# Attention branch rebuilt around half-wide tables, keys and norm pairs, and GpSimd's mixer arithmetic on VectorE

## The chip, the cores and the metric

One core of one Trainium2 chip runs the whole program. The metric is the device time of one execution in microseconds (us); lower is better. In the profile PE is TensorE, DVE is VectorE, ACT is ScalarE, POOL is GpSimd and SP is SyncE, which issues the DMAs.

## What is computed

A trunk of two layers over 1024 tokens of width 1024, all in float32. Cut to what matters here:

```python
z = rmsnorm(h, g_attn) @ w_in           # one projection, feeds three mixers
a = gmlp(z[0:512])                      # chunked, 4 heads
b = attention(q=z[512:1024], k, v)      # 8 query heads, 2 key heads, window 128, sinks
c = s5_ssm(z[1280:1536])                # complex scan, then a gated unit
h = h + concat(norm(a), norm(b), norm(c)) @ w_out
h = h + relu(rmsnorm(h, g_mlp) @ w_ff1)**2 @ w_ff2
h = h + sigmoid(rmsnorm(h, g_ple) @ w_ple_gate) * (p[i] @ w_ple_proj)

def attention(q, k, v):
    q, k = rope(rmsnorm(q, gq)), rope(rmsnorm(k, gk))
    s = masked(q @ k.T / 8)             # the block's own 128 keys and the 128 before
    m = max(max(s), sink)
    pr = exp(s - m)
    return (pr / (sum(pr) + exp(sink - m))) @ v
```

## The kernel before

The 1024 tokens are worked on as two halves (h = 0, 1) of 512. A stage set (l, h) is layer l of half h: `project`, then the three mixers `attention`, `ssm` and `gmlp`, then `mix_out` (the w_out product, L1182), then the window. `window(l, h)` (L1218) is the channel MLP followed by the product with w_ple_gate; between the two it calls `embedding` (L1305), which loads and transposes p. Every wide product runs as three passes over values split in two parts (hi and lo); `load_w` (L93) makes such a pair of weights: a DMA into `st`, a cast on ACT (L104) and a subtraction on DVE (L105). `split_scaled` (L87) makes a pair of activations: ACT writes hi (L89), DVE writes lo (L90).

The stages are generators (`lane`). While a window issues its own matmuls through `main`, the lanes are stepped a fixed number of times per matmul, so that the mixers of the next stage set but one are written into the program between the matmuls of the window (`mix_lane`, L1409). The `until` at L1245 runs the lanes of the next stage set to their end before the second half of the window's last chunk (the w_ff2 product of chunk 7) and `embedding` are written. Tile then orders the instructions of each engine (L1436); on the chip each engine works strictly in that order.

Before the first window there is no such cover. `run` (L1384) projects half 0, starts `gmlp(0,0)` and `attention(0,0)`, projects half 1 as the main work, and finishes `mix_out(0,0)`, which needs all three mixers of half 0. The last reduction of the queries' squares in the projection of half 1 is L685. `early=3` lets three outputs of that `mix_out` begin with the parts that are ready.

`attention` (L946): per block of 128 tokens `rope` builds its two tables from the gains (L992), multiplies by the root and rotates (L993 to L1000), keys in `k_steps`, queries in `q_steps`. A unit is a block and a key head: `attn_q` transposes its queries, `attn_scores`, `attn_softmax`, `attn_pt` and `attn_pv` follow. `attn_norm` (L1158) sums the squares of a finished block on DVE (L1167), adds over partitions with a matmul (L1169), forms the root on DVE in steps of 128 columns (L81 to L85) and multiplies on POOL (L1173); `attn_out` writes the pair of halves into X. `rstd_wide` (L270) is the other way to a root: a matmul with ones, two DVE steps, three rounds of one ACT square and two DVE steps (L281 to L283), all reading a PSUM bank. Its default bank `o` also holds `po` of attention and one of the two `ppt` tiles of `embedding` (L1309).

Of the kernel before, what the change touches and what calls it, by code (L numbers as in the profile page):

```python
# [62 lines left out]
class Trunk:  # L63
# [206 lines left out]
    def rstd_wide(self, sq, count, eps, key, scratch, tag="o"):  # L270


        V, ps = self.V, self.bank(tag)
# [4 lines left out]
        a = pool.tile([P, 512], F32, tag=t, name="rs_a", bufs=bufs)
# [5 lines left out]
        self.R[key] = (None, y)  # L284
# [66 lines left out]
    def setup(self):  # L351
# [42 lines left out]
        self.hf = B.tile([P, 2, 4, 10], F32, name="hf")  # L394
        self.carry = B.tile([P, 2, 2, 4, 1], F32, name="carry")
# [12 lines left out]
    def load_gains(self, t):  # L408
# [9 lines left out]
        Q.dma_start(self.sinks.rearrange("p l a -> p (l a)"), a["sinks"].rearrange("l a -> (l a)").partition_broadcast(P))  # L418

# [249 lines left out]
    def project(self, l, h, ring, tag, one_pass):  # L669
# [35 lines left out]
        self.rsqrt(f, s2, self.small, 40)  # L705
        self.flags.add(("zq", l, h))
# [17 lines left out]
    def ssm(self, l, h, side, tag="p"):  # L724
# [17 lines left out]
        def states(gh):  # L742
# [14 lines left out]
            for ri, (x1, x2, op) in enumerate(((sr, si, ALU.add), (si, sr, ALU.subtract))):  # L757
# [3 lines left out]
                G.tensor_tensor(d1[:, ri, :, 1:65], d1[:, ri, :, 1:65], tm[:, :, 0:64], op)  # L761
# [64 lines left out]
        G.tensor_tensor(gw[:, 1], raw, gw.bitcast(F32)[:, 0], ALU.subtract)  # L826
# [25 lines left out]
        for m in range(2):  # L852
            G.tensor_tensor(yc[m], yc[m], self.R["t"][1], ALU.mult)
# [8 lines left out]
    def gmlp(self, l, h, side, tag="p", after=()):  # L862
# [28 lines left out]
        G.tensor_tensor(x, x, bc(mu), ALU.subtract)  # L891
# [19 lines left out]
        G.tensor_tensor(vg, vg, lng.unsqueeze(1).to_broadcast([P, 4, 256]), ALU.mult)  # L911
        G.tensor_tensor(vg, vg, lnb.unsqueeze(1).to_broadcast([P, 4, 256]), ALU.add)
# [24 lines left out]
        for m in range(2):  # L937
            G.tensor_tensor(u[:, m], u[:, m], self.R["t"][1], ALU.mult)
# [7 lines left out]
    def attention(self, l, h, side):  # L946
# [4 lines left out]
        c = dict(l=l, h=h, at=at, kts={}, qs={}, seen=-1, b0=b0)  # L951
        kv = at.tile([P, nb, 2, 2, 64], F32, name="kv")
        for i in range(nb):
            b = b0 + i
            Q.dma_start(kv[:, i].rearrange("p x a d -> p (x a d)"), self.zg[l][b // 4][b % 4][:, 256:512])
        c["kv"] = kv

        gs = []
        for i, (nm, sc) in enumerate((("q_norm_g", 0.125), ("k_norm_g", 1.0))):
            gt = at.tile([P, 2, 2, 32], F32, name=f"g{i}")  # L960
            g, s = gt[:, 0], gt[:, 1]
# [25 lines left out]
    def rope(self, c, x, f, i, b, n):  # L987

        V, G, at = self.V, self.G, c["at"]
        ta, tb = (at.tile([P, 2, 32], F32, name=f"t{j}", bufs=2) for j in range(2))  # L990
        for t, g, cs in zip((ta, tb), c["gains"][i], (self.cos, self.sin)):
            G.tensor_tensor(t, g, cs[:, b].unsqueeze(1).to_broadcast([P, 2, 32]), ALU.mult)  # L992
        G.tensor_tensor(x, x, f.unsqueeze(2).to_broadcast([P, n, 64]), ALU.mult)  # L993
        t1 = at.tile([P, n, 2, 32], F32, tag="rt1", name="rt1")
        t2 = at.tile([P, n, 2, 32], F32, tag="rt2", name="rt2")
        xb = x.rearrange("p h (a d) -> p h a d", a=2)
        G.tensor_tensor(t1, xb, ta.unsqueeze(1).to_broadcast([P, n, 2, 32]), ALU.mult)
        for s in range(2):
            V.tensor_tensor(t2[:, :, s], xb[:, :, 1 - s], tb[:, s].unsqueeze(1).to_broadcast([P, n, 32]), ALU.mult)
        V.tensor_tensor(xb, t1, t2, ALU.add)  # L1000

    def k_steps(self, c):

        V, S, G, T, at = self.V, self.S, self.G, self.T, c["at"]
        for i in range(c["kv"].shape[1]):
            b = c["b0"] + i
            k = c["kv"][:, i, 0]
            self.rope(c, k, self.hf[:, b // 4, b % 4, 8:10], 1, b, 2)
            kst = at.tile([P, 2, 2, 2, 64], F32R, name="kst")
            hi = kst[:, :, 0, 0]  # L1010
            S.copy(hi, k)
            V.tensor_tensor(kst[:, :, 0, 1], k, hi.bitcast(F32), ALU.subtract)
            V.tensor_tensor(kst[:, :, 1, 0], k, hi.bitcast(F32), ALU.subtract)
            S.copy(kst[:, :, 1, 1], k)
            yield
            pk = self.ps.tile([P, 512], F32, tag="t", name="pk")
            for j in range(4):
                T.matmul(pk[:, j * P:(j + 1) * P], kst[:, j // 2, j % 2].rearrange("p a d -> p (a d)"), self.identr,
                         start=True, stop=True)

            kt = at.tile([P, 2, 2, 2, P], F32R, name="kt", bufs=2)
            S.copy(kt[:, :, :, 1], pk.rearrange("p (g s c) -> p g s c", g=2, s=2))
            if i:
                S.copy(kt[:, :, :, 0], c["kts"][b - 1].bitcast(F32)[:, :, :, 1])
            c["kts"][b] = kt

    def q_steps(self, c):
        qs = []

        def load():  # L1030
            q = c["at"].tile([P, 8, 64], F32, name="q", bufs=2)
# [4 lines left out]
        load()  # L1036
        yield
        for i in range(4):
            self.rope(c, qs[i], self.hf[:, c["h"], i, 0:8], 0, 4 * c["h"] + i, 8)
            c["qs"][4 * c["h"] + i] = qs[i]  # L1040
            if 0 < i < 3:
                load()
            yield

    def attn_steps(self, c, kl, ql):

        h, at = c["h"], c["at"]
# [27 lines left out]
        while late:  # L1075
            blk = late.pop(0)[1]
            self.attn_out(c, blk, o.pop(blk))

    def attn_q(self, c, blk, gk):
        V, S, T, at = self.V, self.S, self.T, c["at"]  # L1080
        qh = c["qs"][blk][:, gk * 4:gk * 4 + 4]
        qst = at.tile([P, 4, 2, 64], F32R, name="qst")
        S.copy(qst[:, :, 0], qh)
# [356 lines left out]
```

## Time and profile before

| what | value |
|---|---|
| median of 3 runs | 2416.62 us (2414.51 to 2419.43) |
| the profiled execution | 2412.62 us, span 2410.8 us, granted clock 0.991 |
| PE busy | 2333.5 us, 97% of the span, 10957 instructions |
| DVE busy | 1604.0 us, 67% |
| ACT busy | 1025.4 us, 43% |
| POOL busy | 288.7 us, 12%, 313 instructions |
| DMA queue of SP | 39.4% of 16 engines' span |

The profile is of one execution. Busy time is a sum over the whole span; a stage can have another limit than the whole. An idle time in front of an instruction is listed with the event that ended it. The row of the granted clock tells at which of its levels TensorE ran.

### The profile page before, as it was taken

To read this page: it belongs to the slowest core of one execution; us is meant where nothing else is said; L and a number is where in the kernel's file an instruction comes from. 1 tells how busy PE (TensorE), PEld (TensorE's weight loads), DVE (VectorE), ACT (ScalarE), POOL (GpSimd) and SP (SyncE) were. 2 spreads that over 40 slices of the span, in tenths; PEclk is the share of its full clock that TensorE was granted. 3 is DMA by queue.
4 is the path that set the end of the run, shared out by engine and by line. 5 is a ranking of instruction groups with operands and counts; after the bars stand their busy time and mean duration, and the time that the engine had idled before them with its cause. 6 is when DMAs were issued, how large, how long until landed. Compare 5 with 4: busy or idle time off the path is not lost. (4 is left out here: it accounts for less than half of the span.)

```text
span 2410.8 us, 29899 instructions
## 1 busy us (share of the span) xinstructions
PE 2333.5 (97%) x10957; PEld 1882.7 (78%) x10957; DVE 1604.0 (67%) x2741; ACT 1025.4 (43%) x1813; POOL 288.7 (12%) x313
## 2 busy tenths in 40 slices
PE   7879999999999999999999999999999999999999
PEld 6656777887788887778788787778878878888887
DVE  7899798658666647876766764777575754444464
ACT  7357465334344434643433543553343533222242
POOL 0642321101000003211010001311010000000000
PEclk9989999999999999999999999999999999999999
DMA  7665522534533244234333335325343333333232
GB/s 236 191 184 149 158 82 79 162 97 139 158 96 114 89 148 127 83 111 148 111 124 102 103 111 152 108 71 162 99 122 115 102 103 109 97 97 96 88 114 71
DMA packets 407212, 289.71 MB, mean 120 GB/s; under 512 B 74668, under 2 KB 384792, under 8 KB 405272
## 3 DMA queue, kind: packets, MB, share of 16 engines
q1 hardware_dynamic: 407064, 287.78, 39.4%
q8 instruction: 87, 1.43, 0.2%
q14 instruction: 61, 0.50, 0.1%
HBM read 252.58 MB, written 35.15 MB: 119 GB/s over the span
## 5 line engine op out<-in xcount | busy, mean ns | idle before, releaser
L104 ACT CAST w<-st 128x1024 fp32r<-128x1024 f32 x384 | 410.4, 1070 | 841.7 <-PE mm_ps L344 441.2
L344 PE MATMUL mm_ps<-x,w 128*128 128x512 f32 x2736 | 666.7, 396 | 10.4 <-DVE hss L685 3.8
L105 DVE TENSOR_TENSOR w<-st,w 128x1024 fp32r<-128x1024 f32 x384 | 494.0, 1288 | 188.5 <-ACT w L104 181.9
L344 PEld LDWEIGHTS mm_ps<-x,w 128*128 128x128 f32 x2736 | 513.7, 189 | 129.0 <-issue 13.8
L344 PE MATMUL mm_ps<-A,w 128*128 128x512 f32 x2016 | 505.3, 394 | 4.2 <-DVE H L1228 3.0
L344 PEld LDWEIGHTS mm_ps<-A,w 128*128 128x128 f32 x2016 | 375.4, 188 | 90.4 <-issue 5.5
L344 PE MATMUL x_ps<-A,w 128*128 128x512 f32 x1056 | 276.7, 395 | 4.8 <-DVE H L1228 3.6
L344 PE MATMUL s_ps<-x,w 128*128 128x512 f32 x1056 | 253.4, 391 | 4.5 <-DVE w L105 3.2
L344 PEld LDWEIGHTS x_ps<-A,w 128*128 128x128 f32 x1056 | 195.7, 188 | 52.8 <-DVE H L1228 7.6
L344 PEld LDWEIGHTS s_ps<-x,w 128*128 128x128 f32 x1056 | 197.7, 188 | 49.6 <-DVE w L105 4.9
L344 PE MATMUL x_ps<-x,w 128*128 128x512 f32 x960 | 232.3, 392 | 0.0
L344 PEld LDWEIGHTS x_ps<-x,w 128*128 128x128 f32 x960 | 179.0, 188 | 38.3 <-issue 1.3
L1228 DVE TENSOR_TENSOR H<-H,mm_ps 128x512 f32<-128x512 f32 x168 | 113.6, 683 | 95.8 <-PE mm_ps L344 94.8
L1239 DVE SCALAR_TENSOR_TENSOR r<-mm_ps,rbc 128x512 f32<-128x512 f32 x88 | 60.6, 689 | 114.4 <-PE mm_ps L344 114.1
L1228 DVE TENSOR_TENSOR H<-H,x_ps 128x512 f32<-128x512 f32 x88 | 60.2, 684 | 76.2 <-PE x_ps L344 76.1
L1243 DVE TENSOR_TENSOR A<-q,A 128x512 fp32r<-128x512 f32 x128 | 92.4, 722 | 1.8 <-ACT q L1242 1.2
L1241 ACT ACTIVATE A<-r 128x512 fp32r<-128x512 f32 x128 | 80.3, 628 | 23.0 <-DVE r L1239 22.6
L695 PE MATMUL s_ps<-w,x 128*128 128x512 f32 x288 | 76.5, 402 | 2.8 <-ACT x L89 1.8
L1242 ACT ACTIVATE q<-r 128x512 f32<-128x512 f32 x128 | 78.9, 617 | 0.0
L313 ACT ACTIVATE nsq<-H 128x512 f32<-128x512 f32 x70 | 44.0, 628 | 58.1 <-DVE H L1280 22.2
L1122 ACT ACTIVATE pr<-pr,anm 128x128 f32<-128x128 f32 x128 | 49.8, 392 | 40.5 <-DVE anm L1119 40.5
L695 PEld LDWEIGHTS s_ps<-w,x 128*128 128x128 f32 x288 | 54.5, 192 | 15.1 <-ACT x L89 2.3
(388 smaller groups left out, 2579.3 us busy)
## 6 DMA issues: line engine op xcount, KB each, us to landing
st<-in_w_ff SPq DMA_DIRECT2D x256, 512.0 KB, 3.9
st<-in_w_out SPq DMA_DIRECT2D x32, 512.0 KB, 3.7
st<-in_w_ple_gate SPq DMA_DIRECT2D x32, 512.0 KB, 3.8
st<-in_w_in SPq DMA_DIRECT2D x28, 512.0 KB, 3.8
st<-in_w_in SPq DMA_DIRECT2D x36, 256.0 KB, 3.8
p<-par SPq DMA_DIRECT2D x8, 1024.0 KB, 7.8
H<-hs SPq DMA_DIRECT2D x4, 2048.0 KB, 8.5
p<-par SPq DMA_DIRECT2D x8, 902.0 KB, 6.5
```

Of the source, the lines that this page charges most:

```text
L104: self.S.copy(hi, src)
L105: self.V.tensor_tensor(lo, src, hi.bitcast(F32), ALU.subtract)
L313: self.S.activation(s, H[:, k], AF.Square)
L344: self.T.matmul(ps, w[:, i, k, c0:c0 + P], X[:, j, k, :], start=(start and n == 0), stop=(stop and n == last))
L695: T.matmul(pss[b], X[:, j, 2 * s + kk, c], w[:, i, kk, :], start=(s == 0 and kk == 0 and n == 0), stop=(s == 3 and kk == 1 and n == 2))
L1122: S.activation(pr[:, i], pr[:, i], AF.Exp, bias=nm[:, i:i + 1], accum_out=den[:, i:i + 1])
L1228: V.tensor_tensor(H[:, m], H[:, m], ps, ALU.add)
L1239: V.scalar_tensor_tensor(r, ps, 0.0, self.R[h][1], ALU.max, ALU.mult)
L1241: S.activation(A[:, 0, m], r, AF.Square)
L1242: S.activation(q, r, AF.Square)
L1243: V.tensor_tensor(A[:, 1, m], q, A.bitcast(F32)[:, 0, m], ALU.subtract)
```

## The change

`attention` builds two tables (cosine or sine times gain) for all its blocks on DVE. All keys of a half are multiplied by their root and rotated in one go; they are transposed into one tile `kT`, and the copy of the preceding block's keys is gone. Keys and values are loaded apart. The queries are rotated 512 wide, without their root: the root goes into the exponential as its `scale`, with the negated root (`nhf`) and the negated sinks (`nsk`) in the shift. The output norm is made for two blocks at once: `attn_sum` adds the squares of a block in two additions, `attn_rstd` calls `rstd_wide` on 256 columns in bank `t`, `attn_out` multiplies 1024 wide and splits 256 wide. Every POOL multiplication, addition and subtraction of the three mixers is on DVE. The tables of the poles (L244 to L252) stay on POOL. In the whole program DVE goes from 2743 to 2686 instructions, POOL's two-input operations from 298 to 36, ACT from 1655 to 1617, the SP queue's DMAs from 843 to 837; the matmuls go from 10445 to 10437.

```diff
+    def rstd_wide(self, sq, count, eps, key, scratch, tag="o", dst=None):
+        n = sq.shape[-1]
+        V, ps = self.V, self.bank(tag)[:, 0:n]
...
-        G.tensor_tensor(tn, wv[:, 1], (tsn, tcs)[ri], ALU.mult)
+        V.tensor_tensor(tn, wv[:, 1], (tsn, tcs)[ri], ALU.mult)
...
-        G.tensor_tensor(vg, vg, lng.unsqueeze(1).to_broadcast([P, 4, 256]), ALU.mult)
+        V.tensor_tensor(vg, vg, lng.unsqueeze(1).to_broadcast([P, 4, 256]), ALU.mult)
...
+            tab = at.tile([P, 2, n, 2, 32], F32, name=f"tab{i}")
+            for j, (x, cs) in enumerate(((g, self.cos), (s, self.sin))):
+                V.tensor_tensor(tab[:, j], x.unsqueeze(1).to_broadcast([P, n, 2, 32]),
+                                cs[:, c0:c0 + n].unsqueeze(2).to_broadcast([P, n, 2, 32]), ALU.mult)
...
         ql = self.q_steps(c)
         next(ql)
+        for i, _ in enumerate(self.k_steps(c)):
+            if i == 1:
+                next(ql)
+            yield
+        yield from self.attn_steps(c, ql)
...
     def k_steps(self, c):
+        V.tensor_tensor(k, k, f.unsqueeze(3).to_broadcast([P, nb, 2, 64]), ALU.mult)
...
+        V.tensor_tensor(k, k, tc.rearrange("p b a d -> p b (a d)").unsqueeze(2).to_broadcast([P, nb, 2, 64]), ALU.mult)
+        V.tensor_tensor(k, k, t2, ALU.add)
...
     def attn_steps(self, c, ql):
                 if gk == 1:
-                    o[blk] = self.attn_norm(c)
-                    late.append((p, blk))
+                    yield from self.wait(("z", c["l"], h))
+                    self.attn_sum(c, blk)
+                    if blk % 2:
+                        late.append((p, blk - 1, self.attn_rstd(c)))
...
     def attn_softmax(self, c, blk, gk, scores):
+        V.tensor_reduce(nm, pr, AX.X, ALU.max)
+        V.tensor_tensor(nm, nm, nf, ALU.mult)
+        V.tensor_tensor(nm, nm, self.nsk[:, c["l"], hs], ALU.min)
...
+            S.activation(pr[:, i], pr[:, i], AF.Exp, bias=nm[:, i:i + 1], scale=f[:, i:i + 1],
+                         accum_out=den[:, i:i + 1])
...
-        G.tensor_tensor(pr, pr, den.unsqueeze(2).to_broadcast([P, 4, P]), ALU.mult)
+        V.tensor_tensor(pr, pr, den.unsqueeze(2).to_broadcast([P, 4, P]), ALU.mult)
...
+    def attn_sum(self, c, blk):
+        S.copy(c["o"][:, b], po)
+        sq = at.tile([P, 4, P], F32, tag="rt1", name="osq")
         S.activation(sq, po, AF.Square)
-        V.tensor_reduce(s, sq.rearrange("p a q -> p q a"), AX.X, ALU.add)
+        V.tensor_tensor(sq[:, 0:2], sq[:, 0:2], sq[:, 2:4], ALU.add)
+        V.tensor_tensor(c["os"][:, b], sq[:, 0], sq[:, 1], ALU.add)
...
+    def attn_rstd(self, c):
+        r = c["at"].tile([P, 256], F32, tag="k", name="or")
+        self.rstd_wide(c["os"].rearrange("p b q -> p (b q)"), 512, EPS, None, (c["at"], "rt2", 1), "t", r)
...
+    def attn_out(self, c, blk, r):
+        V.tensor_tensor(o, o, r.rearrange("p (b q) -> p b q", b=2).unsqueeze(2).to_broadcast([P, 2, 4, P]), ALU.mult)
+        x = lambda i, m: X[:, i, 2 + m, blk % 4 * P:(blk % 4 + 2) * P].rearrange("p (b q) -> p b q", b=2)
         for m in range(4):
+            self.split_scaled(x(0, m), x(1, m), o[:, :, m], self.g_mix(c["l"], 2 + m))
```

The order of the matmuls moves at two places that count. The first is PE at the end of `attention(0,0)`, where `mix_out(0,0)` begins. Before (x_437 is the input of the projection of half 1, x_1443 the input of `mix_out`, `os` the squares of the output norm, `ssq` those of the ssm):

```order
L1156 MATMUL po<-pc,vd 64x256 x2
L344 MATMUL mm_ps<-x_437,w 128x512 x10
L837 MATMUL x_ps<-y_1472,gw 128x512 x6
L344 MATMUL mm_ps<-x_437,w 128x512 x12
L1169 MATMUL t_ps<-os,onesr 128x128
L344 MATMUL mm_ps<-x_437,w 128x512 x8
L837 MATMUL x_ps<-y_1472,gw 128x512 x6
L344 MATMUL mm_ps<-x_437,w 128x512 x20
L344 MATMUL mm_ps<-x_1443,w 128x512 x6
L274 MATMUL x_ps<-ssq,onesr 128x512
L344 MATMUL mm_ps<-x_1443,w 128x512 x6
```

With the change (x_1432 is the input of `mix_out` there):

```order
L346 MATMUL mm_ps<-x_1432,w 128x512 x6
L346 MATMUL s_ps<-x_1432,w 128x512 x5
L843 MATMUL x_ps<-y_1451,gw 128x512 x6
L1154 MATMUL po<-pp,v 64x256 x2
L1154 MATMUL po<-pc,vd 64x256 x2
L275 MATMUL x_ps<-ssq,onesr 128x512
L275 MATMUL t_ps<-os,onesr 128x256
L346 MATMUL mm_ps<-x_1432,w 128x512 x4
L346 MATMUL s_ps<-x_1432,w 128x512 x2
```

Before, 28 matmuls of the projection, six of the ssm's gated unit and six of `mix_out` follow the last norm's matmul; now the matmuls of `mix_out` that read the attention's output follow it at once.

The second is PE at the end of window (1,0). Before (x_12736 is the input of `mix_out(1,1)`, x_10153 that of the window's own w_ff1 product, `nacc` the squares of the stream of half 1, `ptk` the token-major p, `A` the input of w_ff2):

```order
L344 MATMUL s_ps<-x_12736,w 128x512 x47
L344 MATMUL mm_ps<-A,w 128x512 x7
L344 MATMUL x_ps<-A,w 128x512 x12
L344 MATMUL mm_ps<-x_10153,w 128x512 x34
L274 MATMUL o_ps<-nacc,onesr 128x512
L344 MATMUL mm_ps<-x_10153,w 128x512 x14
L344 MATMUL x_ps<-x_10153,w 128x512 x24
L344 MATMUL mm_ps<-x_10153,w 128x512 x24
L344 MATMUL mm_ps<-A,w 128x512 x8
L344 MATMUL x_ps<-A,w 128x512 x2
L1314 MATMUL ppt<-identr,ptk 128x128 x4
```

With the change (x_12310 is the input of `mix_out(1,1)`):

```order
L346 MATMUL mm_ps<-A,w 128x512 x3
L346 MATMUL s_ps<-x_12310,w 128x512 x95
L275 MATMUL o_ps<-nacc,onesr 128x512
L1315 MATMUL ppt<-identr,ptk 128x128 x8
L346 MATMUL x_ps<-A,w 128x512
L346 MATMUL mm_ps<-A,w 128x512
L346 MATMUL s_ps<-pT,w 128x512 x2
L346 MATMUL x_ps<-A,w 128x512 x11
```

Before, 53 matmuls stand between the last one of `mix_out(1,1)` and the sum of its squares, and 72 between that and the first transposes of p. Now none stands at either place, and all eight transposes stand together ahead of the last chunk's w_ff2 product.

## Rows read from the trace of the kernel before

**Rows 1.** The page, part 1: busy time, share of the span and instructions by engine.
```profile
PE 2333.5 (97%) x10957; PEld 1882.7 (78%) x10957; DVE 1604.0 (67%) x2741; ACT 1025.4 (43%) x1813; POOL 288.7 (12%) x313
```

**Rows 2.** Windows of the span: length, then PE, PEld, DVE, ACT, POOL busy, PEclk, DMA.
```profile
60.00:120.00 60.00, 48.94 (x225) 38.44 (x223) 51.57 (x89) 22.81 (x36) 41.67 (x52) 0.91 0.65 190
120.00:180.00 60.00, 41.71 (x262) 34.14 (x261) 56.14 (x119) 34.69 (x91) 27.91 (x25) 0.83 0.63 184
180.00:250.00 70.00, 64.85 (x329) 47.68 (x329) 65.50 (x137) 47.40 (x107) 16.01 (x13) 0.93 0.51 152
300.00:350.00 50.00, 47.00 (x241) 38.13 (x240) 47.81 (x93) 33.28 (x77) 15.06 (x20) 1.00 0.35 105
1870.00:1930.00 60.00, 60.00 (x267) 49.13 (x266) 43.39 (x59) 31.82 (x47) 0.00 (x0) 1.00 0.31 97
```

**Rows 3.** Timeline at 231 us: start, duration, instruction, idle before it and releaser.
```profile
231.32 1.27 DVE L685 TENSOR_REDUCE hss<-mm_ps 128x8 f32<-128x512 f32 x2
...
232.05 1.65 PE L344 MATMUL mm_ps<-x,w 128*128 128x512 f32 x3 [3.79 <-DVE hss L685]
```

**Rows 4.** Windows: from attention's first table to L685, and around that wait.
```profile
105.00:232.00 127.00, 102.34 (x587) 79.74 (x586) 119.33 (x245) 80.94 (x191) 51.00 (x52) 0.89 0.61 183
...
225.00:231.00 6.00, 2.73 (x15) 1.86 (x13) 6.00 (x12) 6.00 (x11) 1.04 (x1) 1.00 0.51 131
231.00:238.00 7.00, 5.95 (x14) 4.70 (x15) 7.00 (x22) 3.63 (x13) 1.46 (x1) 0.53 0.73 191
```

**Rows 5.** Timeline at 131 us: a POOL instruction and the DVE one beside it.
```profile
131.06 1.90 POOL L891 TENSOR_TENSOR vg<-vg,lmu 128x1024 f32<-128x1024 f32 x1 [5.71 <-DVE lmu L889]
...
131.21 1.77 DVE L1119 TENSOR_SCALAR anm<-am 128x4 f32<-128x4 f32 x1
```

**Rows 6.** Groups by form, POOL and DVE: count, busy us, mean ns, idle before.
```profile
L1128 POOL TENSOR_TENSOR pr<-pr,aden 128x512 f32<-128x512 f32 x32 | 37.4, 1168 | 160.4 <-DVE aden L1127 102.3 <-ACT pr L1111 13.1 <-ACT qt L1090 10.8
...
L907 DVE TENSOR_TENSOR vg<-vg,lrs 128x1024 f32<-128x1024 f32 x4 | 4.9, 1214 | 0.1
...
L84 DVE TENSOR_TENSOR rs_a<-rs_a,rs_y 128x4 f32<-128x4 f32 x12 | 2.0, 168 | 0.2
```

**Rows 7.** Timeline from attention(0,0)'s last norm to the first window.
```profile
259.15 0.38 PE L1169 MATMUL t_ps<-os,onesr 128*128 128x128 f32 x2
...
265.35 0.29 DVE L85 SCALAR_TENSOR_TENSOR or<-rs_a,rs_y 128x128 f32<-128x128 f32 x1
...
268.99 1.95 PE L344 MATMUL mm_ps<-x,w 128*128 128x512 f32 x6
...
317.58 0.72 PE L344 MATMUL mm_ps<-x,w 128*128 128x512 f32 x2 [0.41 <-ACT x L89]
```

**Rows 8.** Timeline at the end of window (1,0), by engine: PE, DVE, ACT, SP's queue.
```profile
1875.65 5.60 PE L344 MATMUL s_ps<-x,w 128*128 128x512 f32 x24
...
1893.19 1.02 PE L274 MATMUL o_ps<-nacc,onesr 128*128 128x512 f32 x2
...
1881.29 0.69 DVE L1205 TENSOR_TENSOR H<-H,s_ps 128x512 f32<-128x512 f32 x1 [3.30 <-PE s_ps L344]
...
1887.89 0.68 DVE L314 TENSOR_TENSOR nacc<-nacc,nsq 128x512 f32<-128x512 f32 x1
...
1894.25 0.70 DVE L275 TENSOR_SCALAR o_ps<-o_ps 128x512 f32<-128x512 f32 x1 [0.22 <-PE o_ps L274]
...
1896.43 0.69 DVE L282 SCALAR_TENSOR_TENSOR rs_a<-rs_a,o_ps 128x512 f32<-128x512 f32 x1 [0.76 <-ACT rs_a L281]
1897.16 0.69 DVE L283 SCALAR_TENSOR_TENSOR rbc<-rs_a,rbc 128x512 f32<-128x512 f32 x1
...
1881.29 4.41 ACT L89 ACTIVATE x<-H,gT 128x512 fp32r<-128x512 f32 x7 [4.03 <-PE s_ps L344]
...
1907.24 0.38 SPq L98 DMA_DIRECT2D st<-in_w_ff  x1
...
1911.77 1.05 ACT L104 CAST w<-st 128x1024 fp32r<-128x1024 f32 x1 [0.56 <-DMA st<-in_w_ff]
```

More of the change, by code (lines that the diff above doesn't have):

```diff
@@ L910, in gmlp @@
             self.gelu2(u[:, m], u[:, m], gm, 512, "ggelu", 1)
[L911 to L912 removed]
+        V.tensor_tensor(vg, vg, lng.unsqueeze(1).to_broadcast([P, 4, 256]), ALU.mult)
+        V.tensor_tensor(vg, vg, lnb.unsqueeze(1).to_broadcast([P, 4, 256]), ALU.add)
         yield
@@ L950, in attention @@
         nb = 4 + h
[L951 to L961, printed above, removed]
+        c = dict(l=l, h=h, at=at, qst={}, b0=b0, nb=nb)
+        k = at.tile([P, nb, 2, 64], F32, tag="k", name="k")
+        v = at.tile([P, nb, 2, 64], F32, name="v")
+        for x, c0 in ((k, 256), (v, 384)):
+            if h:
+                Q.dma_start(x[:, 0].rearrange("p a d -> p (a d)"), self.zg[l][0][3][:, c0:c0 + P])
+            Q.dma_start(x[:, h:].rearrange("p b a d -> p b (a d)"),
+                        self.zg[l][h][:, :, c0:c0 + P].rearrange("b p c -> p b c"))
+        c["k"], c["v"] = k, v
+        gt = at.tile([P, 2, 2, 2, 32], F32, tag="kst", name="gt")
+        c["tab"] = []
+        for i, (nm, sc, c0, n) in enumerate((("q_norm_g", 0.125, 4 * h, 4), ("k_norm_g", 1.0, b0, nb))):
+            g, s = gt[:, i, 0], gt[:, i, 1]
             Q.dma_start(g.rearrange("p a b -> p (a b)"), a[nm][l].partition_broadcast(P))
@@ L1016, in k_steps @@
             pk = self.ps.tile([P, 512], F32, tag="t", name="pk")
             for j in range(4):
[L1018 to L1024, printed above, removed]
@@ L1025, in k_steps @@
-            c["kts"][b] = kt
+                T.matmul(pk[:, j * P:(j + 1) * P], kst[:, j // 2, j % 2:j % 2 + 2].rearrange("p a d -> p (a d)"),
+                         self.identr, start=True, stop=True)
+            S.copy(c["kT"][:, :, :, i], pk.rearrange("p (g s c) -> p g s c", g=2, s=2))
+            yield
     def q_steps(self, c):
+        V, S, at = self.V, self.S, c["at"]
         qs = []
         def load():
-            q = c["at"].tile([P, 8, 64], F32, name="q", bufs=2)
+            q = at.tile([P, 8, 64], F32, name="q")
@@ L1060, in attn_steps @@
             if late and late[0][0] < p:
-                yield from self.wait(("z", c["l"], h))
-                blk = late.pop(0)[1]
-                self.attn_out(c, blk, o.pop(blk))
+                self.attn_out(c, *late.pop(0)[1:])
             if 0 <= p < n:
                 st[p] = self.attn_softmax(c, *units[p], self.attn_scores(c, *units[p], st[p]))
-                if units[p][1]:
-                    next(kl, None)
             yield
@@ L1074, in attn_steps @@
             yield
-        while late:
-            blk = late.pop(0)[1]
-            self.attn_out(c, blk, o.pop(blk))
     def attn_q(self, c, blk, gk):
[L1080 to L1083, printed above, removed]
-        V.tensor_tensor(qst[:, :, 1], qh, qst.bitcast(F32)[:, :, 0], ALU.subtract)
+        qst = c["qst"][blk]
         pq = self.ps.tile([P, 512], F32, tag="t", name="pq")
         for i in range(4):
-            T.matmul(pq[:, i * P:(i + 1) * P], qst[:, i].rearrange("p a d -> p (a d)"), self.identr, start=True,
-                     stop=True)
-        qt = at.tile([P, 4, P], F32R, name="qt", bufs=2)
-        S.copy(qt.rearrange("p a b -> p (a b)"), pq)
+            self.T.matmul(pq[:, i * P:(i + 1) * P], qst[:, gk * 4 + i].rearrange("p a d -> p (a d)"), self.identr,
+                          start=True, stop=True)
+        qt = c["at"].tile([P, 4, P], F32R, name="qt")
+        self.S.copy(qt.rearrange("p a b -> p (a b)"), pq)
         return qt
     def attn_scores(self, c, blk, gk, qt):
-        kt, out = c["kts"][blk], []
-        k0 = 0 if blk else 1
+        i, out = blk - c["b0"], []
+        i0, k0 = (i - 1, 0) if blk else (i, 1)
         for pair in range(2):
             ps = self.ps.tile([P, 2, 2, P], F32, tag="s", name="pss", bufs=2)
-            for i in range(2):
+            for j in range(2):
                 for sw in range(2):
-                    self.T.matmul(ps[:, i, k0:], qt[:, 2 * pair + i], kt[:, gk, sw, k0:], start=(sw == 0),
+                    self.T.matmul(ps[:, j, k0:], qt[:, 2 * pair + j], c["kT"][:, gk, sw, i0:i + 1], start=(sw == 0),
                                   stop=(sw == 1))
@@ L1152, in attn_pv @@
             c["po"] = self.ps.tile([P, 2, 2, P], F32, tag="o", name="po")
-        for j, v in enumerate((c["kv"][:, max(i0 - 1, 0), 1], c["vd"]) if blk else (c["kv"][:, 0, 1],)):
+        for j, v in enumerate((c["v"][:, max(i0 - 1, 0)], c["vd"]) if blk else (c["v"][:, 0],)):
             for par in range(2):
```

137 lines of the change are left out of this document (57 added, 80 removed).

## The prediction, written before the changed kernel ran

> **What bounds the kernel now.** I read the busy shares first, then windows of the span, then the timeline where PE waits, then the order of the matmuls. PE is busy for 97% of the span [rows 1], so a microsecond is won or lost only where PE idles. From about 320 us on the windows feed it: 60.00 of 60 us at 1870 us with DVE at 43.39 [rows 2]. DVE work added or removed there is hidden as long as no PE instruction waits for it. The first 250 us are another case. There PE has 48.94, 41.71 and 64.85 us in stretches of 60, 60 and 70, and DVE 51.57, 56.14 and 65.50 [rows 2]: DVE is the limit. The plainest sign is at 231 us: PE sits idle for 3.79 us until the last reduction of the queries' squares (L685) has read its bank [rows 3]. That reduction is late because everything before it stood in DVE's queue, so it is the milestone I use. The first window begins when `mix_out(0,0)` is through, at 317.58 us [rows 7].
>
> So there are three places to price: the stretch before the milestone, the end of `attention(0,0)`, and the ends of the windows.
>
> **Part 1, up to the milestone.** From 105 to 232 us DVE runs 245 instructions and is busy 119.33 of 127 us, while POOL is busy 51.00 us [rows 4]. Some of these DVE times are not their own. A `TENSOR_SCALAR` of 128x4 took 1.77 us beside a POOL instruction of 1.90 [rows 5]; a 128x4 DVE instruction has a mean of 0.168 [rows 6]. So nearly all of the POOL instruction, 1.6 of 1.9 us or 84%, was taken from DVE here. Setting each of the 245 instructions against the usual time of its form without POOL beside it, I count 23 us lost. The bounds of the loss are 0 (if the long times have another cause) and 51.00 x 0.84 = 43 us; I take 23, as it goes instruction by instruction. Against it stands what POOL did: a 128x512 multiply for 1.168 us on POOL costs about 0.69 on DVE [rows 6, 8], 128x1024 about 1.21 [rows 6]. Softmax gives 8 such multiplies to a stage set (5.5 us), `gmlp` three of 1024 and two of 512 (5.0), `ssm` eight quarter-wide ones at about 0.42, two of 512 and one of 1024 (6.0): 16.5 us for each stage set. The new rotation, tables and summing give 1.5 back (fewer and wider instructions, two additions for a reduction). Most of this falls behind the milestone: in front of it I count only 2 us net, because there the ropes that shrink stand against `gmlp`'s and softmax's share. The durations of the 245 instructions add up to 137 us against 119.33 busy, so neighbours overlap by 0.07 us each; 27 fewer of them lose 2 us of that. So 23 - 2 - 2 = 19, less up to 5 us of idle that may open: **milestone 17 us earlier** (bounds -4 to 39).
>
> The Trainium skill, page "Perfetto Trace Analysis", section "Optimizing Scalar/DVE Operations", says that work may be moved off a saturated DVE to ScalarE or even GpSimd, and in the same paragraph that DVE and GpSimd share an SBUF port, so moving between those two might not help. The first half speaks against this change: by it the milestone would be later by 2 to 5 us, not earlier. The row of 1.77 us decides for the second half.
>
> **Part 2, the end of attention(0,0).** Because attention and its lanes start later in the order relative to the projection, more PE work is left at the milestone: about 42 us until `mix_out` reads the attention's output, against 37 before (232.05 to 268.99 [rows 3, 7]): +5.
>
> Then the new norm. Before, the last block's norm had its matmul at 259.15 and its root at 265.35, and PE worked on other things until 268.99 [rows 7]: hidden. In the new order the sum's matmul (L275 t_ps<-os) is followed directly by matmuls that need its result. It cannot start before both blocks of the pair are summed. Its chain, from the last `po`: ACT copy and square 1.2, two additions 0.7, the matmul 1.0 [rows 8], then two roots at once (the ssm's, 512 wide, and the pair's, 256 wide) through the same DVE and ACT. 512 wide costs 0.69 a step [rows 8], 128 wide 0.29 [rows 7], so 256 wide about 0.42: first steps 2.2, three rounds of 2.2 = 6.6, the ssm's two multiplies 1.4, the 1024-wide multiply 1.2 [rows 6], the splits in front 2.4 and the first of its own 0.4. Sum 17, less 1 us of PE work: **16 us of PE idle**, bounds 8 (if DVE is free to run the roots side by side) and 20.
>
> After 3.79 us of idle the granted clock was 0.53 for 7 us (231 to 238 us), having been 1.00 before [rows 4]: that is the lower level, 1.2 in place of 2.4 GHz, and costs 0.47 x 7 = 3.4 us. I add 3.4 once after this gap and once after the one in part 3. If the earlier idle at 231 us goes, its own 3.4 goes too; it probably does not, since DVE stays the limit there.
>
> What is left of `mix_out(0,0)` took 268.99 to 317.58, 48.6 us; with the ssm and attention both complete it runs dense in about 42, -6.6. **Early part: -17 + 5 + 16 + 3.4 - 6.6 = +0.8** (range -6 to +8; more, if the 43 us are true).
>
> **Part 3, the ends of the windows.** The new attention lane takes more steps, so the lanes end later against the window's own matmuls. In window (1,0) that exhausts the cover. Before, `mix_out(1,1)` ended in PE's order with its last 24 matmuls at 1875.65 to 1881.09, and the chain behind it ran under 53 matmuls, then 72 more. Now 95 matmuls of `mix_out` are followed by the sum, eight transposes and w_ff2 matmuls whose weights are not there. The transposes share bank `o` with the root, so they wait for its last reading; the loads of p and the w_ff2 weights stand in SP's queue behind the reuse of `ptk` and behind w_ple_proj's subtraction, which stands in DVE's queue behind the root. With the durations of [rows 8], where this was hidden: the stream's addition 0.69 beside the first of the splits, which take ACT 4.41, then the last square (another 0.63) and the sum's addition 0.68: with two hand-overs about 6.2 in all; the matmul 1.02; two first steps 1.4; three rounds of 0.63 + 0.69 + 0.69 = 2.07, 6.2 in all (the first round's DVE steps are at 1896.43 and 1897.16); the subtraction 1.2 [rows 6]; the DMA of the w_ff2 weights from issue to the cast that waited for it, 1907.24 to 1911.77, 4.5 with what was queued; cast 1.05; subtraction 1.2. Sum 6.2 + 1.0 + 1.4 + 6.2 + 1.2 + 4.5 + 1.1 + 1.2 = 22.8, less 2 us in which PE has the transposes and a few matmuls: **21 us idle**, +3.4 for the clock: **+24** (18 to 28; 0 if the weights turn out to be loaded already, which the order of SP's queue excludes).
>
> At the end of window (0,1) eight transposes now stand in two pieces of 2 and 6 where there were 2, 2 and 4 with other work between; two loads of p wait for transposes: **+3.7** (one DMA of 2 to 4 us; 0 to 6).
>
> **Part 4, the other windows.** The stalls there are few: 300 to 350 us has PE at 47.00 of 50 with DVE at 47.81 [rows 2], the fullest stretch. Without POOL's interference (POOL still 15.06 busy there) DVE gains as much as it gets: **-3** (-6 to 0).
>
> The removed transposes, copies of keys and DMAs are hidden under PE; they count nothing, and would count nothing even if the cover went, since each is under 1 us. The exponential with `scale` as a pointer is ACT work, and ACT is 43% busy [rows 1].
>
> **Sum.** +0.8 + 24 + 3.7 - 3 = +25.5. The profiled execution took 2412.62, so 2438; the median of the runs is 4.0 above it, so 2442 on that footing. I give 2441.
>
> **The rivals.** (a) *Faster: DVE's relief is much larger than I count.* If POOL really holds DVE for 84% of its 51 us, the milestone comes 43 us earlier less the 2 + 2 of part 1, so 39 and not 17, -22; and the windows' stalls before L105 and the like shrink by 10 rather than 3, -7. 25.5 - 29 = -3.5; if the early chain then also shortens to 8 us, as DVE is free to run it, -8 more: 2405 on the median's footing. It decides from a relief of about 47 us in all. For it: the 1.77 row. Against it: counted instruction by instruction the loss is 23, not 43. Chance 0.09.
> (b) *No change: the chain of part 3 stays hidden*, because the last squares are summed before the splits and the loads are issued while `mix_out(1,1)` still runs, so that PE idles only for the root's few us: with 24 down to some 2, and with 3.7 halved, +1 to +3: 2418. Chance 0.12.
> (c) *Slower still: DVE gets no relief.* The long DVE times have another cause, so the milestone is 4 us later instead of 17 earlier. Then 25.5 + 21 = +46, 2463; half of it 2452. For it: DVE at 94% in 105 to 232 us; against it: the 1.77 row. Chance 0.12. (The rule of the Trainium skill's page "Perfetto Trace Analysis", section "Optimizing Scalar/DVE Operations", in its first half, would give this.)
> (d) *The change does less than it says*: nothing to test; every moved instruction is in the order.
>
> **How the numbers follow.** My forecast (2430 to 2450) has 0.67, the rivals 0.09, 0.12 and 0.12. The likeliest is 2441. Eight times in ten the range is 2414 to 2458: it takes in (b) and half of (c), and leaves out (a) and the rest. A measurement of this kernel tells about 0.2%, 4.8 us, from no change: faster means under 2411.8, slower over 2421.4. Faster is (a), 0.09; same is (b) less its upper end, 0.10; slower the rest, 0.81.
>
> **What would show it.** In the profile of the changed kernel: the last reduction of the queries' squares ends near 215 us; PE idle of 10 us or more before the first w_out matmul that reads the attention's output, with the root's round as releaser; the first window's first matmul near 318; granted clock about 0.5 for some 7 us after both gaps; about 21 us of PE idle near 1.9 ms, ended by a w_ff2 weight's cast. POOL's busy time falls from 288.7 to some 40 us, and no DVE 128x4 instruction over 0.5 us after 100 us. It is wrong if the chain near 1.9 ms is absent, if PE is dense between 250 and 320 us, or if DVE's time for the same forms has not fallen.

## The result and the profile after

The changed kernel takes 2437.1 us (median of 4 runs, 2434.86 to 2438.83), the kernel before 2418.0 beside it: a ratio of 1.008, interval 1.0062 to 1.0097, so 19 us slower. The profiled execution took 2438.83; that of before, 2412.62, was one of its fastest, so the two traces lie 26 us apart, 7 more than the medians.

Part 1 of the page of the changed kernel, which answers to [rows 1]:

```profile
PE 2337.6 (96%) x10941; PEld 1891.7 (78%) x10941; DVE 1575.9 (65%) x2684; ACT 1032.4 (42%) x1775; POOL 35.0 (1%) x51
```

VectorE took over nearly all of GpSimd's work and is busy for 28 us less than before, not more. PE's busy time is nearly the same (2337.6 against 2333.5 us). The windows of the changed kernel (length, then PE, PEld, DVE, ACT, POOL, clock, DMA):

```profile
105.00:232.00 127.00, 108.98 (x601) 87.27 (x600) 108.34 (x231) 80.25 (x171) 0.96 (x1) 0.85 0.64 190
...
1900.00:1990.00 90.00, 72.60 (x302) 57.20 (x300) 57.69 (x78) 35.48 (x50) 0.00 (x0) 0.87 0.28 82
```

and one of the kernel before:

```profile
1900.00:1990.00 90.00, 88.25 (x401) 72.17 (x400) 57.79 (x78) 37.58 (x55) 0.00 (x0) 1.00 0.39 114
```

From 105 to 232 us VectorE is relieved: 108.34 us against 119.33 [rows 4]. At 1.9 ms PE does 302 matmuls in the 90 us in which it did 401. What PE waited for in all, from the waits of the changed kernel (waited for, total us, times, longest):

```profile
PE mm_ps L346 <- ACT x L89: 11.9, 2, 11.7
PE ppt L1315 <- DVE rs_a L283: 10.6, 2, 7.0
PE ppt L1315 <- DMA ptk<-in_p: 7.4, 3, 3.1
PE o_ps L275 <- DVE nacc L316: 6.2, 1, 6.2
```

In the kernel before, the first of these comes to 1.0 us and the other three are not among PE's waits at all. The first is the output norm ahead of `mix_out(0,0)`; the others are the ends of windows (0,1) and (1,0). The timeline of PE at those places:

```profile
263.56 0.70 PE L275 MATMUL t_ps<-os,onesr 128*128 128x256 f32 x2
276.01 2.08 PE L346 MATMUL mm_ps<-x,w 128*128 128x512 f32 x4 [11.75 <-ACT x L89]
...
321.39 0.73 PE L346 MATMUL mm_ps<-x,w 128*128 128x512 f32 x2 [0.15 <-ACT x L89]
...
1364.30 0.69 PE L1315 MATMUL ppt<-identr,ptk 128*128 128x128 f32 x2 [3.63 <-DVE rs_a L283]
1368.12 1.12 PE L1315 MATMUL ppt<-identr,ptk 128*128 128x128 f32 x4 [3.13 <-DMA ptk<-in_p]
...
1931.00 2.08 PE L275 MATMUL o_ps<-nacc,onesr 128*128 128x512 f32 x2 [6.17 <-DVE nacc L316]
1932.87 0.42 PE L1315 MATMUL ppt<-identr,ptk 128*128 128x128 f32 x1
1940.25 0.91 PE L1315 MATMUL ppt<-identr,ptk 128*128 128x128 f32 x3 [6.97 <-DVE rs_a L283]
1942.86 0.69 PE L1315 MATMUL ppt<-identr,ptk 128*128 128x128 f32 x2 [1.70 <-DMA ptk<-in_p]
1946.10 0.69 PE L1315 MATMUL ppt<-identr,ptk 128*128 128x128 f32 x2 [2.55 <-DMA ptk<-in_p]
1946.79 0.80 PE L346 MATMUL x_ps<-A,w 128*128 128x512 f32 x1
```

The idle of the last stretch adds up to 6.17 + 6.97 + 1.70 + 2.55 = 17.4 us. The same events of both traces show where the 26 us come in:

| event | before | after | later by | added in the stretch |
|---|---|---|---|---|
| window (0,0), first matmul | 317.58 | 321.39 | 3.8 | 3.8 |
| projection (1,0), first matmul | 838.18 | 839.87 | 1.7 | -2.1 |
| projection (1,1), first matmul | 1414.46 | 1425.72 | 11.3 | 9.6 |
| first transpose of the output | 1961.31 | 1988.63 | 27.3 | 16.1 |
| end of the span | 2410.8 | 2437.1 | 26.3 | -1.0 |

The third stretch holds the end of window (0,1), the fourth that of window (1,0).

### The profile page after: what moved, and what is told of

It is laid out like the page before. It is cut to its first block, busy times and chain, and to the rows that moved or that the text cites. A ratio compares the mean times of both kernels' runs of the same rounds, so it can differ in the third digit from the quotient of the medians.

```text
span 2437.1 us, 29296 instructions
## 1 busy us (share of the span) xinstructions
PE 2337.6 (96%) x10941; PEld 1891.7 (78%) x10941; DVE 1575.9 (65%) x2684; ACT 1032.4 (42%) x1775; POOL 35.0 (1%) x51
## 5 line engine op out<-in xcount | busy, mean ns | idle before, releaser
L105 DVE TENSOR_TENSOR w<-st,w 128x1024 fp32r<-128x1024 f32 x384 | 475.2, 1239 | 216.5 <-ACT w L104 214.9
L346 PE MATMUL mm_ps<-A,w 128*128 128x512 f32 x2016 | 499.3, 392 | 0.7 <-DVE H L1229 0.7
L1119 ACT ACTIVATE pr<-pr,anm,hf 128x128 f32<-128x128 f32 x128 | 61.6, 484 | 17.7 <-DVE anm L1116 17.7
```

What stands on the lines that cost most here:

```text
L105: self.V.tensor_tensor(lo, src, hi.bitcast(F32), ALU.subtract)
L346: self.T.matmul(ps, w[:, i, k, c0:c0 + P], X[:, j, k, :], start=(start and n == 0), stop=(stop and n == last))
L1119: S.activation(pr[:, i], pr[:, i], AF.Exp, bias=nm[:, i:i + 1], scale=f[:, i:i + 1], accum_out=den[:, i:i + 1])
```

## The experiments

Theory A: the loss is at the two window ends, where the lanes of the next stage set come too late in PE's order to cover the chain, and the move from GpSimd to VectorE gains. Rival B: VectorE's added work costs. Rival C: the exposed output norm of `attention(0,0)` costs most. Each kernel was timed beside the kernel before on one chip; a ratio is to that, with its interval. Where an experiment gains or loses is read from the third and fourth stretch of the table above, in the profiled executions (us; e4, e6 and e8 move the first transpose of the output in the order and are left out):

| kernel | projection (1,0) to projection (1,1) | projection (1,1) to output |
|---|---|---|
| before | 576.3 | 546.9 |
| changed | 585.9 | 562.9 |
| e1 | 579.5 | 560.3 |
| e2 | 569.9 | 543.8 |
| e3 | 579.0 | 555.0 |
| e9 | 582.2 | 563.0 |
| e11 | 568.5 | 543.8 |
| e12 | 574.9 | 552.1 |

**e1, GpSimd back, and e2, GpSimd off alone.** e1 is the changed kernel with nine lines of this kind turned back; e2 is the kernel before with all of them turned, in attention, ssm and gmlp:

```diff
-        V.tensor_tensor(pr, pr, den.unsqueeze(2).to_broadcast([P, 4, P]), ALU.mult)
+        self.G.tensor_tensor(pr, pr, den.unsqueeze(2).to_broadcast([P, 4, P]), ALU.mult)
```

> The changed kernel with the multiplications of softmax, ssm and gmlp back on GpSimd (nine lines), the rest of the change kept. Theory A (the loss sits at the ends of windows (0,1) and (1,0), where the lanes come too late to cover, and VectorE gained by the move): DVE instructions beside POOL get long again, the milestone of the first phase comes about 10 us later, and the end of window (1,0) loses some 8 us less because the lanes stand 10 us earlier in PE's order: 2437 to 2447. Rival B (the loss is VectorE's added work): the loss goes, 2415 to 2422.

> The kernel before with every multiplication and addition of the three mixers moved from GpSimd to VectorE, and nothing else changed. Theory A: VectorE's instructions lose their long times, the first phase ends 5 to 15 us earlier; mix_out(1,1) ends 10 us later in PE's order but still before the window's own products run out, so little of the end of window (1,0) opens (0 to 8 us): 2403 to 2418. Rival B (VectorE's added work costs): 2425 to 2440.

e1: 2438.7 us, 1.0082 (1.0069 to 1.0096), as the changed kernel. e2: 2405.2 us, 0.9951 (0.9938 to 0.9964), 12 us faster than before. Rival B falls: the loss is not the moved arithmetic. The move alone gains, and the rebuilt attention costs some 32 us against it (2437.1 to 2405.2). In e1, with the rebuilt attention and GpSimd busy for 166.0 us in place of 35.0, the move of these nine lines is worth nothing: projection (1,0) starts at 847.5 us, 7.6 later than in the changed kernel, but projection (1,1) at 1427.0, only 1.3 later, and the first transpose of the output at 1987.3, 1.3 earlier. What GpSimd costs in the first stages it gives back at the window ends, where its lanes lie closer. The windows of e2, as above:

```profile
100.00:200.00 100.00, 78.19 (x445) 62.83 (x445) 92.04 (x244) 59.75 (x142) 0.96 (x1) 0.85 0.67 203
...
1900.00:1990.00 90.00, 89.02 (x405) 72.42 (x404) 59.42 (x80) 38.28 (x55) 0.00 (x0) 1.00 0.38 113
```

The end of window (1,0) is full there, at 405 matmuls. VectorE is as busy as ever in the first phase (92.04 us), and the gain is not made there but in the third and fourth stretch: projection (1,0) of e2 starts at 840.9 us, 2.7 later than before, projection (1,1) at 1410.8, 3.7 earlier, the first transpose of the output at 1954.6, 6.7 earlier.

**e3, keys spread.** The rebuilt attention transposes all keys ahead of its first query; e3 takes two blocks (three in half 1), and the others between units (and gives `os` the buffer of a table, no longer that of `kst`):

```diff
-        for i, _ in enumerate(self.k_steps(c)):
+        kl = self.k_steps(c)
+        for i in range(3 + h):
+            next(kl)
...
+                if units[p][1]:
+                    next(kl, None)
```

> The changed kernel with the keys' transposes spread as before: two blocks (three in half 1) ahead of the first query, the others between the units; the keys are still multiplied and rotated all at once. Theory A: the lanes stand about 20 us earlier in PE's order at the end of window (1,0), the chain there is covered but for some 5 us, the first phase loses 3 to 5 us less: 2412 to 2424. Rival B (VectorE's work) and rival C (the exposed norm of attention(0,0) is the main loss): 2432 to 2440, as the changed kernel.

2422.3 us, 1.0021 (1.0012 to 1.0029): 15 us of the loss are the order of the keys, and the profiled executions place them: e3 is 6.8 us shorter in the third stretch and 7.9 in the fourth. PE in the changed kernel (`pk` transposes keys, `pq` the first queries):

```profile
1528.05 0.56 PE L1015 MATMUL pk<-identr,kst 128*128 128x128 f32 x4
1537.49 0.55 PE L1015 MATMUL pk<-identr,kst 128*128 128x128 f32 x4
1543.64 0.56 PE L1015 MATMUL pk<-identr,kst 128*128 128x128 f32 x4
1550.26 0.56 PE L1015 MATMUL pk<-identr,kst 128*128 128x128 f32 x4
1556.42 0.56 PE L1015 MATMUL pk<-identr,kst 128*128 128x128 f32 x4
1561.90 0.56 PE L1083 MATMUL pq<-identr,qst 128*128 128x128 f32 x4
```

in e3:

```profile
1521.80 0.56 PE L1017 MATMUL pk<-identr,kst 128*128 128x128 f32 x4
...
1537.15 0.56 PE L1017 MATMUL pk<-identr,kst 128*128 128x128 f32 x4
1543.09 0.56 PE L1087 MATMUL pq<-identr,qst 128*128 128x128 f32 x4
...
1910.28 1.02 PE L275 MATMUL o_ps<-nacc,onesr 128*128 128x512 f32 x2
```

and in the kernel before:

```profile
1521.05 0.72 PE L1018 MATMUL pk<-identr,kst 128*128 128x128 f32 x4 [0.36 <-DVE kst L1012]
1526.70 0.56 PE L1087 MATMUL pq<-identr,qst 128*128 128x128 f32 x4
```

Each further block comes some 6 us after the one before it (the second 9). By the program they share one `kst` buffer and one bank and go through ACT and VectorE between window work; which of these sets the 6 us was not tested. Behind the queries comes everything else of the lane. Counted from the first matmul of projection (1,1), the first queries are transposed after 136.2 us in the changed kernel, 124.8 in e3 and 112.2 before, and the squares of `mix_out(1,1)` are summed on PE after 505.3, 492.0 and 478.7 us: the order of the keys is half of the lateness. Hardly any PE time is lost here; it is lost 370 us later, where `mix_out(1,1)` and its chain end after the window's own matmuls.

**e4 and e9, the embedding.** e4 puts the second transposed tile into bank t and the loads of w_ple_proj behind the last w_ff2 product; e9 has the first edit alone:

```diff
-        pts = [self.ps.tile([P, 512], F32, tag="po"[k], name="ppt") for k in range(2)]
+        pts = [self.ps.tile([P, 512], F32, tag="pt"[k], name="ppt") for k in range(2)]
```

> The changed kernel with two edits in the embedding alone: its second transposed tile in bank t instead of o, and the loads and splits of w_ple_proj behind the last w_ff2 product instead of ahead of it. Theory A, with the bank and the loads as what the end of the window waits for: end of window (0,1) gets back 8 to 11 us, end of window (1,0) 6 to 14, as the w_ff2 product can run while the root is formed: 2412 to 2424. If the wait there is something else: 2432 to 2440.

> The changed kernel with one word changed: the embedding's second transposed tile in bank t instead of o; the loads of w_ple_proj stay where they were. In e4 the root of the window's end came late (the multiply gt waited 9 us for it in window (0,1)), which I put down to the loads moved behind the w_ff2 product. If so, the bank alone gives back more at the end of window (0,1) than e4 (10 to 12 us of the 13) and little at the end of window (1,0) (0 to 4): 2421 to 2429. If the wait on gt comes from the bank: about 2432 as e4.

e4: 2432.1 us, 1.0062 (1.005 to 1.0075). e9: 2434.6 us, 1.0062 (1.005 to 1.0075). Both missed the gain expected: e4 came to the time named for the case that the wait is something else, e9 near the one named for a wait on `gt` that comes from the bank. The bank gives back 2 to 5 us, not 13, and the intervals overlap that of the changed kernel. Where the wait for the root goes, another takes its place; from the waits of e9:

```profile
PE ppt L1315 <- DMA ptk<-in_p: 11.5, 2, 9.8
...
PE o_ps L275 <- DVE nacc L316: 6.2, 1, 6.2
PE p_ps L346 <- DVE gt L1278: 5.9, 1, 5.9
```

In window (0,1) PE now waits for the multiply `gt`, which needs the root in any case; that stretch is 3.6 us shorter than in the changed kernel. In window (1,0) it waits for the last load of p, and nothing is won. That load stands in SP's queue behind one of w_ff2 weights, which waits until the subtraction of w_ple_proj, itself behind the root on VectorE, has freed a buffer:

```profile
1936.85 0.69 DVE L284 SCALAR_TENSOR_TENSOR rbc<-rs_a,rbc 128x512 f32<-128x512 f32 x1
1937.46 2.35 DVE L105 TENSOR_TENSOR w<-st,w 128x1024 fp32r<-128x1024 f32 x2
...
1938.71 0.38 SPq L98 DMA_DIRECT2D st<-in_w_ff  x1
1939.18 0.45 SPq L1313 DMA_DIRECT2D ptk<-in_p  x1
```

So the bank is one of several parallel waits of the same stretch.

**e5, norm by blocks.** The changed kernel with the root and the multiply for each block of 128, on VectorE:

```diff
-        self.rstd_wide(c["os"].rearrange("p b q -> p (b q)"), 512, EPS, None, (c["at"], "rt2", 1), "t", r)
+        self.T.matmul(ps, self.ones, s, start=True, stop=True)
+        V.tensor_scalar(s, ps, 1.0 / 512.0, EPS, ALU.mult, ALU.add)
+        self.rsqrt(r, s, at, P)
```

> The changed kernel with the attention's output norm formed for each block of 128 tokens again (root in steps of 128 columns on VectorE, multiply and split per block), all on VectorE, the rest kept. Rival C (the pair's norm, exposed in front of mix_out(0,0), is a main part of the loss): the 12 us of idle there shrink to 4 to 8 and the time to 2426 to 2432. Theory A (the lanes' lateness at the ends of two windows is the main part): only 3 us, 2432 to 2437, since the lanes come just 3 us earlier there.

2442.1 us, 1.0093 (1.0078 to 1.0108): outside both expected ranges and no gain; the loss of 3 to 5 us is not clear of the noise, as the intervals overlap. The wait before `mix_out(0,0)` falls from 11.7 to 9.6 us, but 2.0 us in front of the norm's matmul join it. Rival C falls: the idle there is real, but it costs little (the first window starts 3.8 us later), and the pairs are not its cause. e2, with the old norm, has 8.2 us there, behind the matmul that sums the squares of the ssm; attention's last sum is 17 us earlier:

```profile
251.20 0.38 PE L1169 MATMUL t_ps<-os,onesr 128*128 128x128 f32 x2
...
267.92 1.02 PE L274 MATMUL x_ps<-ssq,onesr 128*128 128x512 f32 x2
...
278.77 2.08 PE L344 MATMUL mm_ps<-x,w 128*128 128x512 f32 x4 [8.21 <-ACT x L89]
```

**e6, e8, e10, e12, edits together.** e6 is e3 with e4; e8 is e6 with e5; e10 is e3 with e9; e12 is e10 with e5.

> The changed kernel with the edits of the runs e3 and e4 together. Theory A (the two window ends hold what is left of the loss): of the 25 us of idle left at the two ends in e3 about 17 are more than in the kernel before, and 8 to 15 of them go: 2407 to 2414. If what is left in e3 is lost elsewhere (first phase, queries): 2418 to 2424.

> The changed kernel with the edits of e3, e4 and e5 together: keys spread, norm by blocks, embedding's bank and loads. What stays of the rebuilt attention is the tables, the queries rotated 512 wide and the root in the exponential. Theory A: 2402 to 2412, at least level with e2 within 5 us. If the tables, the wide queries or the exponential cost time: 2415 to 2425.

> e3 (keys spread) with the bank alone. With the loads left in place the end of window (0,1) should have no more idle than in the kernel before (11 down to about 4 us) and the end of window (1,0) 10 to 14 as in e3: 2411 to 2418. If the bank does nothing once the lanes are early: 2420 to 2424.

> e8 with the loads of w_ple_proj left where the changed kernel has them: keys spread, norm by blocks, bank t. Against e11 it differs only by what is left of the rebuilt attention: tables built once, loads of keys and values apart, queries 512 wide, root in the exponential, two additions for a reduction. e10 against e6 says that the late loads cost about 4 us, so 2408 to 2412; if it comes to 2402 to 2406, what is left of the rebuild costs nothing against e11, if it comes to 2413 or more, the rest of the rebuild costs 10 us or so.

e6: 2423.4 us, 1.0022 (1.0013 to 1.0031); e8: 2414.0, 0.9981 (0.9971 to 0.9991); e10: 2419.1, 1.0003 (0.9992 to 1.0014); e12: 2417.2, 0.9998 (0.9989 to 1.0007). None of the four came as far as expected. Together the edits take back 14 to 23 of the 32 us, but do not add up: e5 gains nothing alone and 9 us in e8 against e6. Each edit moves the whole order, so differences of a few us between these four say nothing of one edit. In e12 the rest of the rebuilt attention stands 14 us behind e11 (below). The profiled executions have it in the same two places, 6.4 us more in the third stretch and 8.4 in the fourth, and the largest new wait is still that of a window end (9.1 us in three waits for loads of p). So where the 14 us are lost is known; which part of the rebuild loses them stays open.

**e7, work on GpSimd that nobody needs.** e2 with six multiplications of 128x128 in each unit of attention on a tile that nothing reads, 192 in all (to make room, the two half tables of the rotation have one buffer in place of two):

```diff
+        for _ in range(6):
+            self.G.tensor_tensor(self.idle, self.idle, m[:, 0:1].to_broadcast([P, 128]) if _ == 0 else self.idle, ALU.mult)
```

> The kernel of e2 (before, with the mixers' work on VectorE) with six multiplications of 128x128 on GpSimd added to each unit of attention, 192 in all, on a tile of their own that nobody reads (the two half tables of the rotation have one buffer instead of two to make room). Theory A (GpSimd takes VectorE's time while it runs): the VectorE instructions beside them get long again (128x4 instructions over 0.5 us), total VectorE time up by 20 us or more, the time up by 3 to 10 us, 2408 to 2415. Rival D (the move gained by shorter chains only): VectorE's times as in e2, 2403 to 2407.

2411.1 us, 0.9972 (0.9962 to 0.9983): 6 us slower than e2. GpSimd is busy for 111.1 us more, and VectorE's busy time rises from 1621.7 to 1638.6 us, 17 where at least 20 were expected. The same instruction in e2 and in e7 (count, busy us, mean ns):

```profile
L1119 DVE TENSOR_SCALAR anm<-am 128x4 f32<-128x4 f32 x32 | 5.3, 167 | 0.5
```
```profile
L1123 DVE TENSOR_SCALAR anm<-am 128x4 f32<-128x4 f32 x32 | 8.4, 262 | 0.5
...
L1121 DVE TENSOR_TENSOR am<-am,sinks 128x4 f32<-128x4 f32 x32 | 6.9, 216 | 4.3 <-POOL idle L1119 4.3
```

So GpSimd lengthens VectorE's instructions without giving it any result. Of the 6 us a part may be plain waiting: the last row shows 4.3 us in which VectorE waited for a buffer that the added work still read, and what the single buffer of the half tables costs was not measured. Nor does e7 say how much of e2's 12 us is VectorE's relief, and how much comes from the moved steps being shorter there (the multiply of the softmax, 128x512, takes 0.687 us on VectorE in e2 and 1.168 on GpSimd before).

**e11, the faster version.** e2 with the edit of e9.

> e2 (the kernel before with the mixers' work on VectorE) with the bank alone. In e2 the two window ends hold 4 and 5 us of idle, about as in the kernel before, so there is little to win: 2401 to 2407. It is run as the version that may beat both kernels.

2403.3 us, 0.9936 (0.9923 to 0.9949): 15 us faster than before and 34 faster than the changed kernel.

## Why the prediction was right, and which steps were not

The forecast of 2441 us met 2437.1, and +25.5 on the profiled execution met +26.2; between the medians 19.1 us stand against the 24.4 forecast. The terms did less well than their sum. Early part, window (0,1), window (1,0) and the rest were given +0.8, +3.7, +24 and -3; the stretches of the event table add 3.8, 9.6, 16.1 and -3.1. One term was 8 us too large and two together 9 too small, so that the sum came out so close is luck; that there was a loss of this kind at these places is not.

**Part 1: right in kind, half in size.** The last reduction of the queries' squares ends at 224.3 us, not 232.6: 8 earlier, where I said 17. In e2, where only GpSimd's work has moved, it ends at 229.3, 3 earlier, and with e7's added work at 233.1; in e1, with nine lines back, at 229.4. So the move gives 3 us of the 8 alone and some 5 with the rebuilt attention.

```profile
223.64 0.68 DVE L690 TENSOR_REDUCE hss<-mm_ps 128x8 f32<-128x512 f32 x1
```

e7 shows that GpSimd lengthens VectorE's instructions, and the same form of 128x4 fell in mean from 208 ns before to 159 in the changed kernel:

```profile
L1126 DVE TENSOR_TENSOR aden<-aden,aes 128x4 f32<-128x4 f32 x32 | 6.7, 208 | 12.1 <-ACT aes L1125 12.0
```
```profile
L1124 DVE TENSOR_TENSOR aden<-aden,aes 128x4 f32<-128x4 f32 x32 | 5.1, 159 | 14.3 <-ACT aes L1123 14.3
```

The one row of 1.77 us was the extreme case: in e7 111.1 us of GpSimd's work took 17 us from VectorE, 15% and not 84%. The second half of the rule in the Trainium skill, page "Perfetto Trace Analysis", section "Optimizing Scalar/DVE Operations" (moving work between the two might not help, as they share a port) agrees with the ratio of e2, 0.9951; by its first half e2 would have been slower.

**Part 2: right in kind.** The norm ahead of `mix_out(0,0)` leaves PE idle for 1.15 + 11.75 = 12.9 us (I said 16, from 8 to 20), and the first window starts 3.8 us later (I said 0.8). What is left of `mix_out(0,0)` behind it took 45.4 us (276.01 to 321.39), not 42. I had both roots in the sum; e2 and e5 show that the gap stays without the pair's.

**Part 3, window (1,0): right in place, too large, wrong in its reason.** From the last matmul of `mix_out(1,1)` (1924.86, when VectorE adds) to the first w_ff2 matmul (1946.79) the chain takes 21.9 us; I had 22.8 (22.6 with the round added up rightly: 0.63 + 0.69 + 0.69 is 2.01, not 2.07). Idle is 17.4, not 21, because PE's few matmuls took 4.5 us of the chain and not 2, the sum of squares 2.08 in place of 1.02, at the lower clock. With the 1.8 us that the clock cost behind the gap (last section) this makes 19 and not 24, and 19.1 is what the fourth stretch has more than in e2, where the same work is on VectorE and the end is covered. The last wait ended with a load of p and not with the cast of a w_ff2 weight, but the two came together; the first w_ff2 matmul starts at 1946.79:

```profile
1945.69 1.04 ACT L104 CAST w<-st 128x1024 fp32r<-128x1024 f32 x1 [4.33 <-DMA st<-in_w_ff]
```

The step that failed is "the new attention lane takes more steps": by the program it takes 44 in place of 43. What makes the lane late is latency, half of it the order of the keys (e3: 15 us of the total); the other half stays open.

**Part 3, window (0,1): the term was mis-sized.** I gave +3.7 (0 to 6) for one late load; the stretch adds 9.6 us, and 16.0 against e2. Its transposes too wait for a root in bank `o` (3.63 us) and for loads (3.13 us) while no other matmul is left. It is the chain of window (1,0) again, and I had looked only at the number of transposes.

**Part 4: too small, the other way.** I gave -3 for all windows. Between the first matmuls of window (0,0) and of projection (1,0) alone 2.1 us are won, and e2 shows what the move from GpSimd is worth where the ends stay covered: 12 us, with 6.4 and 3.0 of it in the third and fourth stretch. In the changed kernel that gain is hidden in the two ends' losses.

Rival (a) asked for a relief of 47 us and is out. Rival (b) is out: the chain near 1.9 ms lies open. Rival (c), no relief, is refuted by the milestone, 8 us earlier (3 in e2) and not 4 later, by the shorter instructions of part 1, and by e7.

## What to carry to other kernels

Work that only feeds a later stage can lose time without ever idling the bound engine near it: look where the stage ends against the work that was to cover its end, and count the microseconds of cover left. Gathering small steps (all keys, then all queries) saves instructions and lengthens the way to the first result; here the engines it saved were not the bound, and the trade cost 15 us. Move single-engine edits and restructurings apart: here the one was worth -12 us alone, and the other +32 on top of it.

## What the hardware showed that I had not expected

PE was busy without a break from 1918 to 1924 us at a granted clock of 1.00; then come the gaps of the chain, in which the clock falls to 0.50, the lower level, and it stays there in the first work behind them. Windows of the changed kernel, and below them those behind the gap ahead of `mix_out(0,0)`:

```profile
1918.00:1924.00 6.00, 6.00 (x28) 4.89 (x28) 3.12 (x4) 1.13 (x2) 0.00 (x0) 1.00 0.00 0
1924.00:1931.00 7.00, 0.82 (x5) 0.36 (x3) 6.07 (x10) 5.53 (x9) 0.00 (x0) 0.74 0.00 0
1931.00:1940.00 9.00, 2.29 (x3) 0.73 (x3) 5.25 (x8) 2.41 (x4) 0.00 (x0) 0.50 0.00 1
1940.00:1947.00 7.00, 2.49 (x8) 1.29 (x9) 3.39 (x5) 2.67 (x4) 0.00 (x0) 0.50 0.58 183
1947.00:1951.00 4.00, 4.00 (x10) 3.14 (x11) 3.33 (x4) 1.76 (x3) 0.00 (x0) 0.50 0.42 121
1951.00:1955.00 4.00, 4.00 (x18) 3.26 (x18) 0.07 (x1) 1.05 (x1) 0.00 (x0) 0.97 0.57 152
```
```profile
276.00:279.00 3.00, 2.99 (x7) 2.43 (x8) 3.00 (x7) 2.09 (x4) 0.00 (x0) 0.50 0.36 90
279.00:282.00 3.00, 3.00 (x8) 2.35 (x8) 3.00 (x11) 0.00 (x0) 0.00 (x0) 0.50 0.27 81
282.00:286.00 4.00, 4.00 (x18) 3.25 (x18) 3.10 (x7) 1.05 (x1) 0.00 (x0) 0.99 0.23 71
```

10 matmuls in 4 us against 18 in the next 4 show the price, about 8 x 0.23 = 1.8 us; most of the time at 1.2 GHz fell on idle and cost nothing. Behind the other gap 15 matmuls in 6 us, at a pace of 18 in 4 afterwards, make 12 x 0.23, about 2.7 us. I had 3.4 us for each gap (0.47 x 7 is 3.3).
